# Low parts of the weights ahead of the experts: all made by VectorE (DVE), none by GpSimd

## The chip, the cores and the metric

The kernel runs on one core of one Trainium2 chip. The metric is the device time of one execution in microseconds (us). Before the change it is 2900.98 us, the median of 3 runs (2897.74 to 2901.92).

## The reference

Two transformer blocks are computed in fp32 on 256 tokens of width 2048. The first block is a Conformer-like mixer (convolution of width 31, chunked attention, attention to a memory) and a gated feed-forward layer with a short convolution. The second has four kinds of sparse attention and a mixture of 16 experts. Cut to the products with large weights:

```
proj = rmsnorm(x) @ w_in                       # 2048 x 12288
conv = silu(layernorm(dwconv31(a * sigmoid(g))))
merged = g0*(conv @ w_conv_out) + g1*(att @ w_attn_out) + g2*(memory @ w_mem_out)
h  = x + merged @ w_o
up = dwconv3(rmsnorm(h) @ w_up)                # 2048 x 11264
h  = rmsnorm(h + (silu(gt) * val) @ w_down)    # 5632 x 2048
mod = silu(c) @ ada_w + ada_b                  # one row, 2048 x 12288
y = h + g1 * (mixers(norm(h) @ w_in_2) @ w_out_2)
out = norm(y + g2 * experts(norm(y)))          # 16 experts, 2 chosen per token
```

## The kernel before

All weights (some 680 MB) are read once from HBM. TensorE (PE) multiplies in a fast fp32 format (`fp32r`), and the precision of fp32 is kept by splitting: a weight `w` becomes a high part `wh = fp32r(w)` and a low part `wl = w - wh`, an activation likewise `xh`, `xl`, and PE adds up the three products `wh*xh`, `wh*xl`, `wl*xh`.

A product (`Gemm`) is cut into chunks of 128 rows of the weight by up to 1024 columns. Two chunks come with one load of 1 MB, issued by SP into a ring of three buffers. `_split` makes the parts of a chunk: ScalarE (ACT) casts the high part (line 147), and then the low part is a subtraction of two tiles in SBUF (line 149; here called a sub). PE then runs the chunk's matmuls (`_mm`). With the weights as the stationary operand these are 24 matmuls, in lines 183, 184 and 185, the last of them the first to need the low part. In products of the other orientation (`tm`) they are lines 173, 174 and 175, of which 174 needs it.

The order of the work is written by `run`: chunks are split up to `AHEAD` = 4 chunks ahead of the one whose matmuls are issued next. After each chunk, `step` takes one item from each background queue: softmax pieces, convolution taps, evacuations in stages. Every engine runs its instructions in the order in which the program issues them. So the sub of a chunk stands on DVE between the background items of one step and those of the next.

Which engine runs the sub is decided by a counter, `nsplit`, and `pool_share`: every fourth sub of the first block goes to GpSimd (POOL), every third of the feed-forward layer and of the second block's projections, and none from `w_out_2` on (`pool_share` 999), so none in the experts.

Three kinds of work share DVE with the subs. The convolution of width 31 is 8 first taps (line 895) and 240 further ones (line 902), three to a step, each of two SBUF tensors and a column of factors. `ada_w_2` never reaches PE: 96 tiles of it are loaded beside the other weights and each is added up on DVE (line 1151). The feed-forward layer's short convolution (lines 1006 and 1007) and its gate (1046 on POOL, 1053 and 1058 on DVE) are stages of the queue `ev`. Lines 918 to 963 are the layer norm behind the convolution, and line 923 is a matmul of PE that waits for it.

Of the kernel before, what the change touches and what calls it, by code (L numbers as in the profile page):

```python
# [10 lines left out]
F32 = mybir.dt.float32  # L11
# [17 lines left out]
class Gemm:  # L29
# [6 lines left out]
    def __init__(self, w, x, evac, kts=None, cols=None, tm=False, before=None, after=None):  # L36
        self.w, self.x, self.evac, self.tm = w, x, evac, tm
        self.kts = list(range(w.shape[0] // 128)) if kts is None else list(kts)
        self.c0, self.c1 = cols if cols else (0, w.shape[1])
        self.C = self.c1 - self.c0  # L40
        self.before, self.after = before, after
        self.kk = max(1, 2048 // self.C)
        self.banks = None


class Kernel:
    def __init__(self, tc, ins, out, dbg=None):
        self.tc, self.nc, self.i, self.out, self.dbg = tc, tc.nc, ins, out, dbg or {}
        self.chunks, self.pos, self.split_pos, self.nsplit = [], 0, 0, 0
        self.side, self.every, self.count = deque(), None, 0  # L50
        self.rows, self.ahead_only = None, False
        self.loads, self.loaded = [], 0
        self.queues, self.reached = {}, set()
        self.n = 0
# [77 lines left out]
    def _split(self, c):  # L132
        n, off, width = c[:3]
        t, size = self.loads[n]
        wt = t[:, off:off + width]
        if c[3] is None:
            c[4](wt)
            self.free(t)
            return
        if c[7]:  # L140
            c[4], c[6] = wt, t
            return
        self.nsplit += 1
        c[6] = self.U(F32R)
        self.ahead += 1
        wh, wl = c[6][:, 0:1024], c[6][:, 1024:2048]
        self.nc.scalar.copy(wh[:, :width], wt)  # L147
        e = self.nc.gpsimd if self.nsplit % self.pool_share == 0 else self.nc.vector
        e.tensor_sub(wl[:, :width], wt, wh[:, :width].bitcast(F32))  # L149
        c[4], c[5] = wh, wl  # L150
        if off + width == size:
            self.free(t)

    AHEAD, pool_share = 4, 4

    def _mm(self, g, j, wh, wl):
        nc = self.nc
# [820 lines left out]
    def ffn(self):  # L978
# [7 lines left out]

        hid = {}
        NB = (DFF + 1023) // 1024
        self.every, self.pool_share = 3, 3
        self.nsplit = 0  # L990

        fw = i["ffn_conv_w"][0].rearrange("j (t p) -> (j t) p", p=128)
        for j in range(3):
# [254 lines left out]
    def after_ffn(self):  # L1248

        nc = self.nc  # L1250
        if "h1" in self.dbg:
            for tt in range(2):
                nc.sync.dma_start(self.dbg["h1"][tt * 128:tt * 128 + 128, :], self.h[tt])
        self.flush("ev")
        self.flush("norm")
        self.nsplit, self.pool_share = 2, 3
        for kt in range(0, 6, 2):
            self.turn1(kt)
        ss = self.small([128, 4], "ss4")
        nc.vector.tensor_reduce(ss, self.s2.rearrange("p (t k) -> p t k", t=4), axis=AX.X, op=OP.add)  # L1260

        v, zv = ss[:, 0:2], ss[:, 2:4]
        nc.vector.tensor_scalar(ss, ss, 1.0 / D, None, op0=OP.mult)
        nc.vector.tensor_scalar(v, v, EPS, None, op0=OP.add)
        nc.vector.scalar_tensor_tensor(zv, v, EPS, zv, op0=OP.mult, op1=OP.add)
        r = self.small([128, 16], "rstd", 3)
        nc.scalar.activation(r[:, 0:4], ss, AF.Sqrt)
        nc.vector.reciprocal(r[:, 0:4], r[:, 0:4])
        self.R2 = self.spread_tokens(r[:, 2:4])()
        self.parts1(0)  # L1270
        self.parts1(2)
        self.free(*self.h)
        self.free(self.fg)
        self.x = self.hf
        for tt in range(2):
            for c in range(0, D, 512):
                x = self.x[tt][:, c:c + 512]
                self.later("norm", 1 if tt + c else 9, lambda tt=tt, x=x: nc.gpsimd.tensor_scalar(x, x, r[:, tt:tt + 1], None, op0=OP.mult))
# [15 lines left out]
    def mixers(self):  # L1294
# [139 lines left out]
        def rows():  # L1434
            self.flush("ada")
            self.flush("norm")
            half(0)
            self.nsplit, self.pool_share = 0, 999
            self.lg = self.bank()

            self.ring.extend((self.NU, self.NU + 1))

        def begin(c0):
            part[0] = c0
            if c0 == 0:
                rows()
            elif c0 == 1024:
                half(1)

        def half(cb):  # L1450
            M[cb] = self.U()
            for n, k in enumerate((2, 4)):
                nc.gpsimd.dma_start(M[cb][:, n * 1024:n * 1024 + 1024],
                                    self.mod[k:k + 1, cb * 1024:cb * 1024 + 1024].to_broadcast([128, 1024]))
# [321 lines left out]
    def after_mix(self):  # L1776
# [21 lines left out]
        for tt in range(2):  # L1798
            e = slice(tt * 16, tt * 16 + 16)
# [61 lines left out]
        nc.vector.tensor_copy(self.most, most)  # L1861
        self.g2 = self.row(self.mod[5:6, :])
        self.resize(1)
        self.nsplit, self.pool_share = 0, 999

    def logits(self, kt):

# [489 lines left out]
```

## Time and profile before

| What | us |
|---|---|
| median of 3 runs | 2900.98 |
| the profiled execution | 2906.34 |
| its span, first to last instruction | 2904.5 |
| PE busy (matmul) | 2774.8 |
| DVE busy | 2159.3 |
| ACT busy | 1416.9 |
| POOL busy | 905.5 |

Busy times are those of the profiled execution. A matmul's end is modelled, so PE's busy share says where PE had no work rather than how near it is to its peak. Where PE has nothing to do, the view of waits names the line that waited, the line that ended the wait, the total in us, how often, and the longest. The granted clock of TensorE stands in the tables by stage as a share: 1.00 is 2.4 GHz and 0.50 is 1.2 GHz.

### The profile page before, as it was taken

The numbers are of one execution on the slowest core, as the hardware profiler recorded it, in microseconds if no ns is written. First come the engines' busy times: TensorE is split into PE (matmuls) and PEld (weight loads), VectorE is DVE, ScalarE is ACT, GpSimd is POOL, SyncE is SP. The second block draws the span as 40 slices with busy tenths as digits, with TensorE's granted clock in tenths as the row PEclk, the third lists the DMA queues.
The fourth block names the chain that finished last, engine by engine and source line by source line (L and its number), as shares of the span: only waits on it lengthen the run. The fifth ranks groups of instructions, "written<-read, shape, count | busy, mean of one in ns | idle before, by whom it ended". The sixth has DMA issues, their size and how long they took to land. (4 is left out here: it accounts for less than half of the span.)

```text
span 2904.5 us, 44128 instructions
## 1 busy us (share of the span) xinstructions
PE 2774.8 (96%) x17766; PEld 2423.2 (83%) x17766; DVE 2159.3 (74%) x2446; ACT 1416.9 (49%) x2100; POOL 905.5 (31%) x519
## 2 busy tenths in 40 slices
PE   8999999998999999999999999999999899999997
PEld 8898999988998899898989897997886676666664
DVE  5555559999766687887778776746545589998998
ACT  5434444333444444443434444435454476666665
POOL 3322322323344232333333342523221202222223
PEclk9999999999999999999999999989999899999999
DMA  7677654565567674676666674745564699989895
GB/s 253 203 264 233 220 198 163 179 216 198 209 237 270 213 269 171 210 268 215 250 215 249 232 239 156 247 153 191 171 212 154 211 341 340 344 328 343 324 344 212
DMA packets 201428, 685.78 MB, mean 236 GB/s; under 512 B 12147, under 2 KB 15331, under 8 KB 180355
## 3 DMA queue, kind: packets, MB, share of 16 engines
q1 hardware_dynamic: 194336, 662.94, 64.6%
q0 software_dynamic: 5680, 19.53, 2.6%
q8 instruction: 141, 2.31, 0.3%
q10 hardware_dynamic: 1203, 0.45, 0.1%
q14 instruction: 68, 0.56, 0.1%
HBM read 680.66 MB, written 2.20 MB: 235 GB/s over the span
## 5 line engine op out<-in xcount | busy, mean ns | idle before, releaser
L149 DVE TENSOR_TENSOR u<-u,u 128x1024 fp32r<-128x1024 f32 (+3 forms) x831 | 1117.7, 1374 | 406.0 <-ACT u L147 404.5
L147 ACT CAST u<-u 128x1024 fp32r<-128x1024 f32 (+3 forms) x1064 | 1014.3, 995 | 726.2 <-DMA u<-in_w_in_dram 252.4
L149 POOL TENSOR_TENSOR u<-u,u 128x1024 fp32r<-128x1024 f32 (+3 forms) x233 | 582.5, 2500 | 1116.5 <-ACT u L147 1008.4
L185 PE MATMUL ps<-u,u 128*128 128x256 f32 (+1 forms) x2184 | 623.4, 285 | 12.2 <-DVE u L149 9.7
L183 PE MATMUL ps<-u,u 128*128 128x256 f32 (+1 forms) x2184 | 628.3, 288 | 3.3 <-ACT u L147 2.7
L184 PE MATMUL ps<-u,u 128*128 128x256 f32 (+1 forms) x2184 | 622.7, 285 | 0.7 <-DVE u L1290 0.3
L185 PE MATMUL ps<-big,u 128*128 128x256 f32 (+1 forms) x1672 | 479.1, 287 | 17.1 <-DVE u L149 17.1
L183 PE MATMUL ps<-big,u 128*128 128x256 f32 (+1 forms) x1672 | 482.9, 289 | 1.2 <-ACT big L1289 0.7
L184 PE MATMUL ps<-big,u 128*128 128x256 f32 (+1 forms) x1672 | 477.9, 286 | 0.0
L185 PEld LDWEIGHTS ps<-u,u 128*128 128x128 f32 (+1 forms) x2184 | 422.3, 193 | 15.0 <-DVE u L149 11.7
L183 PEld LDWEIGHTS ps<-u,u 128*128 128x128 f32 (+1 forms) x2184 | 422.7, 194 | 12.6 <-issue 6.4
L184 PEld LDWEIGHTS ps<-u,u 128*128 128x128 f32 (+1 forms) x2184 | 422.8, 194 | 2.0 <-DVE u L1290 1.5
L185 PEld LDWEIGHTS ps<-big,u 128*128 128x128 f32 (+1 forms) x1672 | 324.6, 194 | 19.5 <-DVE u L149 19.3
L183 PEld LDWEIGHTS ps<-big,u 128*128 128x128 f32 (+1 forms) x1672 | 324.6, 194 | 13.4 <-issue 8.0
L184 PEld LDWEIGHTS ps<-big,u 128*128 128x128 f32 (+1 forms) x1672 | 324.6, 194 | 0.7 <-DVE big L1290 0.2
L1151 DVE SCALAR_TENSOR_TENSOR u<-u,cols,u 128x2048 f32<-128x2048 f32 x96 | 295.9, 3082 | 18.5 <-DMA u<-in_ada_w_dram 17.0
L174 PE MATMUL ps<-u,u 128*128 128x512 f32 x736 | 290.1, 394 | 15.8 <-DVE u L149 15.8
L173 PE MATMUL ps<-u,u 128*128 128x512 f32 x736 | 293.9, 399 | 1.5 <-ACT u L147 0.4
L175 PE MATMUL ps<-u,u 128*128 128x512 f32 x736 | 288.7, 392 | 0.0
L2135 POOL TENSOR_TENSOR u<-u,ev 128x512 f32<-128x512 f32 x56 | 116.3, 2090 | 418.6 <-DVE ev L2131 418.6
L1920 PE MATMUL ps<-u,xg 128*128 128x512 f32 x416 | 187.9, 452 | 0.4 <-DVE xg L1911 0.3
L174 PEld LDWEIGHTS ps<-u,u 128*128 128x128 f32 x736 | 139.6, 190 | 47.6 <-DVE u L149 20.3
(375 smaller groups left out, 3435.2 us busy)
## 6 DMA issues: line engine op xcount, KB each, us to landing
u<-in_w_in_dram SPq DMA_DIRECT2D x128, 1024.0 KB, 5.1
u<-in_ada_w_dram SPq DMA_DIRECT2D x96, 1024.0 KB, 6.0
u<-in_w_up_dram SPq DMA_DIRECT2D x88, 1024.0 KB, 6.3
u<-in_exp_w_gate_dram SPq DMA_DIRECT2D x64, 1024.0 KB, 9.4
u<-in_exp_w_up_dram SPq DMA_DIRECT2D x64, 1024.0 KB, 6.9
u<-in_exp_w_down_dram SPq DMA_DIRECT2D x64, 1024.0 KB, 8.2
u<-in_w_down_dram SPq DMA_DIRECT2D x44, 1024.0 KB, 6.8
u<-in_w_o_dram SPq DMA_DIRECT2D x16, 1024.0 KB, 6.9
```

Source lines behind the costliest of these rows:

```text
L147: self.nc.scalar.copy(wh[:, :width], wt)
L149: e.tensor_sub(wl[:, :width], wt, wh[:, :width].bitcast(F32))
L173: nc.tensor.matmul(o, xh[:, ts], wh[:, cs], start=first, stop=False)
L174: nc.tensor.matmul(o, xh[:, ts], wl[:, cs], start=False, stop=False)
L175: nc.tensor.matmul(o, xl[:, ts], wh[:, cs], start=False, stop=last)
L183: nc.tensor.matmul(o, wh[:, cs], xh, start=first and m % 2 == 0, stop=False, **kw)
L184: nc.tensor.matmul(o, wh[:, cs], xl, start=False, stop=False, **kw)
L185: nc.tensor.matmul(o, wl[:, cs], xh, start=False, stop=last, **kw)
L1151: nc.vector.scalar_tensor_tensor(a, wt, self.col["c"][:, kt:kt + 1], a, op0=OP.mult, op1=OP.add)
L1920: self.nc.tensor.matmul(ps, x, wh[:, s], start=start, stop=False)
L2135: nc.gpsimd.tensor_add(x, x, st["t"])
```

## The change

The counter, `pool_share` and the choice by them are gone. Every sub is issued on DVE, at the place in the program where it was issued on POOL before.

```diff
@@ _split
-        self.nsplit += 1
         c[6] = self.U(F32R)
         self.ahead += 1
         wh, wl = c[6][:, 0:1024], c[6][:, 1024:2048]
         self.nc.scalar.copy(wh[:, :width], wt)
-        e = self.nc.gpsimd if self.nsplit % self.pool_share == 0 else self.nc.vector
-        e.tensor_sub(wl[:, :width], wt, wh[:, :width].bitcast(F32))
+        self.nc.vector.tensor_sub(wl[:, :width], wt, wh[:, :width].bitcast(F32))
         c[4], c[5] = wh, wl
...
-    AHEAD, pool_share = 4, 4
+    AHEAD = 4
...
@@ ffn
-        self.every, self.pool_share = 3, 3
-        self.nsplit = 0
+        self.every = 3
```

The resets of the two numbers in `__init__`, `after_ffn`, `mixers` and `after_mix` go too. 233 subs move. Nothing else changes its engine or its place in the order. Lines behind the edit have numbers that are 2 to 6 smaller (the sub is line 147 after the change, a tap line 900).

DVE's order in the convolution of width 31, before: `u_4303` is the result that the taps add to, and the rows of line 149 are the subs of two chunks; the chunk between them is POOL's.

```order
L149 TENSOR_TENSOR u_5671<-u_5475,u_5671 128x1024
L902 SCALAR_TENSOR_TENSOR u_4303<-u_4280,cols_1361,u_4303 128x251
L902 SCALAR_TENSOR_TENSOR u_4303<-u_4280,cols_1361,u_4303 128x250
L902 SCALAR_TENSOR_TENSOR u_4303<-u_4280,cols_1361,u_4303 128x249
L902 SCALAR_TENSOR_TENSOR u_4303<-u_4280,cols_1361,u_4303 128x248
L902 SCALAR_TENSOR_TENSOR u_4303<-u_4280,cols_1361,u_4303 128x247
L902 SCALAR_TENSOR_TENSOR u_4303<-u_4280,cols_1361,u_4303 128x246
L149 TENSOR_TENSOR u_5733<-u_5537,u_5733 128x1024
```

The same place on DVE after the change:

```order
L147 TENSOR_TENSOR u_5671<-u_5475,u_5671 128x1024
L900 SCALAR_TENSOR_TENSOR u_4303<-u_4280,cols_1361,u_4303 128x251
L900 SCALAR_TENSOR_TENSOR u_4303<-u_4280,cols_1361,u_4303 128x250
L900 SCALAR_TENSOR_TENSOR u_4303<-u_4280,cols_1361,u_4303 128x249
L147 TENSOR_TENSOR u_5703<-u_5537,u_5703 128x1024
L900 SCALAR_TENSOR_TENSOR u_4303<-u_4280,cols_1361,u_4303 128x248
L900 SCALAR_TENSOR_TENSOR u_4303<-u_4280,cols_1361,u_4303 128x247
L900 SCALAR_TENSOR_TENSOR u_4303<-u_4280,cols_1361,u_4303 128x246
L147 TENSOR_TENSOR u_5733<-u_5537,u_5733 128x1024
```

The sub of `u_5703` stands between the two steps, three taps before it and three behind.

DVE's order in the feed-forward layer, before, ahead of a product with `w_down`: `u_11493` is an evacuated piece, `prob_11516` and `prob_11562` are pieces of the short convolution, `u_10461` the sum over `ada_w_2`.

```order
L1007 SCALAR_TENSOR_TENSOR prob_11516<-u_11493,fcw_1515,prob_11516 128x254
L149 TENSOR_TENSOR u_11542<-u_11426,u_11542 128x1024
L1006 SCALAR_TENSOR_TENSOR prob_11562<-u_11493,fcw_1672,prob_11562 128x255
L1007 SCALAR_TENSOR_TENSOR prob_11562<-u_11493,fcw_1515,prob_11562 128x254
L1006 SCALAR_TENSOR_TENSOR prob_11562<-u_11493,fcw_1672,prob_11562 128x255
L1007 SCALAR_TENSOR_TENSOR prob_11562<-u_11493,fcw_1515,prob_11562 128x254
L149 TENSOR_TENSOR u_11569<-u_11429,u_11569 128x1024
L1151 SCALAR_TENSOR_TENSOR u_10461<-u_11485,cols_1052,u_10461 128x2048
```

The same place on DVE after the change:

```order
L1004 SCALAR_TENSOR_TENSOR prob_11516<-u_11493,fcw_1515,prob_11516 128x254
L147 TENSOR_TENSOR u_11523<-u_11426,u_11523 128x1024
L147 TENSOR_TENSOR u_11542<-u_11426,u_11542 128x1024
L1003 SCALAR_TENSOR_TENSOR prob_11562<-u_11493,fcw_1672,prob_11562 128x255
L1004 SCALAR_TENSOR_TENSOR prob_11562<-u_11493,fcw_1515,prob_11562 128x254
L1003 SCALAR_TENSOR_TENSOR prob_11562<-u_11493,fcw_1672,prob_11562 128x255
L1004 SCALAR_TENSOR_TENSOR prob_11562<-u_11493,fcw_1515,prob_11562 128x254
L147 TENSOR_TENSOR u_11569<-u_11429,u_11569 128x1024
L147 TENSOR_TENSOR u_11584<-u_11429,u_11584 128x1024
L1148 SCALAR_TENSOR_TENSOR u_10461<-u_11485,cols_1052,u_10461 128x2048
```

Two subs (`u_11523`, `u_11584`) came from POOL, each next to a sub that DVE had already.

## Rows read from the trace of the kernel before

**Rows 1.** The page: busy us by engine, then DVE in 40 slices (tenths).

```profile
PE 2774.8 (96%) x17766; PEld 2423.2 (83%) x17766; DVE 2159.3 (74%) x2446; ACT 1416.9 (49%) x2100; POOL 905.5 (31%) x519
...
DVE  5555559999766687887778776746545589998998
```

**Rows 2.** Waits of PE, 585 to 770 us: who for whom: us, times, longest.

```profile
PE ps L185 <- DVE u L149: 18.6, 10, 6.3
PE ps L923 <- DVE ln L918: 5.5, 1, 5.5
PE ps L185 <- POOL u L149: 1.9, 1, 1.9
```

**Rows 3.** Waits of PE, 1115 to 1690 us.

```profile
PE ps L174 <- DVE u L149: 12.3, 10, 1.8
PE ps L185 <- DVE u L149: 6.4, 3, 2.6
```

**Rows 4.** By stretch: length, busy by engine, granted clock, DMA share, GB/s.

```profile
0.00:440.00 440.00, 431.64 (x3097) 400.50 (x3098) 246.06 (x290) 201.12 (x317) 131.73 (x99) 1.00 0.67 227
585.00:770.00 185.00, 158.56 (x1230) 155.52 (x1229) 169.53 (x175) 67.75 (x77) 59.37 (x26) 0.94 0.58 198
1115.00:1260.00 145.00, 135.24 (x900) 124.89 (x900) 120.27 (x108) 63.40 (x79) 50.53 (x23) 0.96 0.65 225
1850.00:2190.00 340.00, 334.80 (x2269) 297.44 (x2267) 187.05 (x391) 165.80 (x375) 103.10 (x89) 0.97 0.58 190
```

**Rows 5.** Stretches at half clock, first one and the sum of eight.

```profile
672.00:678.50 6.50, 3.99 (x18) 3.99 (x19) 6.39 (x6) 0.00 (x0) 4.69 (x2) 0.50 0.47 147
...
sum 32.30, PE 28.70 PEld 27.20 DVE 23.14 ACT 6.54 POOL 14.36; mean PE 3.59 PEld 3.40 DVE 2.89 ACT 0.82 POOL 1.80
```

**Rows 6.** Timeline of DVE, then of POOL: start us, us, line, count.

```profile
563.88 2.53 DVE L902 SCALAR_TENSOR_TENSOR u<-u,cols,u 128x255 f32<-128x255 f32 x1
...
567.47 1.50 DVE L902 SCALAR_TENSOR_TENSOR u<-u,cols,u 128x254 f32<-128x254 f32 x3
...
563.73 2.40 POOL L149 TENSOR_TENSOR u<-u,u 128x1024 fp32r<-128x1024 f32 x1 [1.94 <-ACT u L147]
```

**Rows 7.** Groups by line, 440 to 712 us: busy us, mean ns | idle before.

```profile
L902 DVE SCALAR_TENSOR_TENSOR u<-u,cols,u 128x255 f32<-128x255 f32 (+14 forms) x240 | 163.2, 680 | 6.4
L149 DVE TENSOR_TENSOR u<-u,u 128x1024 fp32r<-128x1024 f32 x57 | 75.0, 1318 | 0.0
...
L149 POOL TENSOR_TENSOR u<-u,u 128x1024 fp32r<-128x1024 f32 x29 | 78.1, 2694 | 182.4 <-ACT u L147 174.4 <-issue 7.9
```

**Rows 8.** Lines 902, 149 (0 to 2200 us), 1151: ns min/median/max.

```profile
L902 DVE SCALAR_TENSOR_TENSOR u<-u,cols,u x240: 449/470/2677, 440.9 to 705.4; 128x255 f32<-128x255 f32 x8, 128x253 f32<-128x253 f32 x8, 128x251 f32<-128x251 f32 x8, 128x249 f32<-128x249 f32 x8
L149 DVE TENSOR_TENSOR u<-u,u x480: 436/1220/3441, 8.4 to 2199.6; 128x1024 fp32r<-128x1024 f32 x139, 128x512 fp32r<-128x512 f32 x14, 128x280 fp32r<-128x280 f32 x4, 128x768 fp32r<-128x768 f32 x3
L1151 DVE SCALAR_TENSOR_TENSOR u<-u,cols,u x96: 2339/2350/4505, 143.4 to 2055.7; 128x2048 f32<-128x2048 f32 x96
```

**Rows 9.** Groups by line, 1115 to 1260 us.

```profile
L149 DVE TENSOR_TENSOR u<-u,u 128x1024 fp32r<-128x1024 f32 x33 | 52.7, 1623 | 15.7 <-ACT u L147 15.6
L1151 DVE SCALAR_TENSOR_TENSOR u<-u,cols,u 128x2048 f32<-128x2048 f32 x8 | 24.9, 3106 | 2.7 <-DMA u<-in_ada_w_dram 2.7
L1006 DVE SCALAR_TENSOR_TENSOR u<-u,fcw,u 128x255 f32<-128x255 f32 x8 | 8.1, 1016 | 0.0
...
L1006 DVE SCALAR_TENSOR_TENSOR prob<-u,fcw,prob 128x255 f32<-128x255 f32 x10 | 7.6, 762 | 5.3 <-ACT prob L1005 5.2
...
L149 POOL TENSOR_TENSOR u<-u,u 128x1024 fp32r<-128x1024 f32 x17 | 47.2, 2778 | 68.6 <-ACT u L147 56.7 <-DVE u L386 8.9 <-issue 3.1
```

**Rows 10.** Waits: DVE in 440 to 712 us, POOL whole span, SP in 440 to 712 us.

```profile
DVE u L447 <- ACT u L446: 0.5, 1, 0.5
...
POOL u L149 <- ACT u L147: 1008.4, 185, 18.0
...
SPq L128 <- DVE u L149: 198.9, 39, 11.5
```

More of the change, by code (lines that the diff above doesn't have):

```diff
@@ L48, in __init__ @@
         self.tc, self.nc, self.i, self.out, self.dbg = tc, tc.nc, ins, out, dbg or {}
-        self.chunks, self.pos, self.split_pos, self.nsplit = [], 0, 0, 0
+        self.chunks, self.pos, self.split_pos = [], 0, 0
         self.side, self.every, self.count = deque(), None, 0
@@ L1255, in after_ffn @@
         self.flush("norm")
-        self.nsplit, self.pool_share = 2, 3
         for kt in range(0, 6, 2):
@@ L1437, in rows @@
             half(0)
-            self.nsplit, self.pool_share = 0, 999
             self.lg = self.bank()
@@ L1863, in after_mix @@
         self.resize(1)
-        self.nsplit, self.pool_share = 0, 999
     def logits(self, kt):
```

## The prediction

> **What bounds the kernel now.** I read the page's busy times first, then the waits of PE by stretch, then the table by stretch with the granted clock, and last the timeline of DVE beside POOL. PE is busy for 2774.8 of 2904.5 us, so it is the engine that ends the kernel, and only time in which it waits, or runs at half clock, can be had back. DVE is second with 74%, but unevenly: its row of 40 slices reaches 9 in the slices of 500 to 700 us [rows 1]. That is the convolution of width 31.
>
> The waits of PE say where DVE is late. From 585 to 770 us PE waits 18.6 us in 10 waits for a sub on DVE, 1.9 us for a sub on POOL, and 5.5 us for the reduction of line 918: 26.0 us [rows 2], the same as the 26.4 us by which PE's busy time misses the stretch (185 less 158.56) [rows 4]. From 1115 to 1690 us, the feed-forward layer, it waits 12.3 us in line 174 and 6.4 us in line 185, both for subs of DVE: 18.7 us [rows 3].
>
> The clock comes on top. Eight stretches, from the one at 672 us to one at 1511.7 us, ran at a granted share of 0.50, which is 1.2 GHz; the first began while PE stood in its longest wait for a sub (6.3 us) and all others lie right behind a wait. PE was busy for 28.70 us in them, work that takes half as long at 2.4 GHz: 14.4 us lost [rows 5]. Four of the eight, 19.5 of their 32.3 us, lie in 585 to 770 us, so I put 8 us there and 6 in the feed-forward layer. (The mean clock of 0.94 over 158.56 us of work would say 9.5 us for the former [rows 4].) Everything that this change can reach is then 26.0 + 18.7 + 14.4 = 59 us.
>
> **The change: what a sub costs on either engine.** On DVE a sub of 128x1024 takes 1.22 us, the median of its line [rows 8]; on POOL it takes 2.69 us in the convolution and 2.78 us in the feed-forward layer [rows 7, 9]. 233 subs move. At 1.22 us each (some are narrower) that is at most 284 us more for DVE, a tenth of the span.
>
> But a sub on POOL isn't free for DVE. At 563.73 us POOL begins one that takes 2.40 us. The tap that DVE begins at 563.88 us takes 2.53 us; three taps at 567.47 us, with nothing on POOL, take 1.50 us together, 0.50 each [rows 6]. So DVE stood still for nearly all of POOL's sub, 2.0 us, which is more than the 1.22 us of doing it itself.
>
> Over the whole convolution (440 to 712 us): 240 taps have a mean of 680 ns and a median of 470, so 50 us is standing still; 57 subs on DVE have a mean of 1318 against 1220, another 6 us. POOL ran 29 subs meanwhile [rows 7, 8]. 56 us by 29 is 1.9 us of DVE's time for each sub that DVE did not do. Moving them takes 56 us away and adds 29 x 1.22 = 35 us: DVE has 21 us less to do.
>
> The Trainium skill ("SBUF — State Buffer", section "Who interferes with whom") says that DVE and GpSimd share one pair of SBUF ports as an exclusive lock, held for a whole instruction, and that a DVE instruction with two SBUF inputs contends with a GpSimd one that reads SBUF. The trace agrees in kind, and is smaller in size: 56 us where the whole of POOL's 78.1 us would be 100%. By the page the relief would be 78.1 - 35 = 43 us, the waits from 585 to 770 us would all go, and the kernel would end near 2858 us.
>
> **What that gives PE, from 585 to 770 us.** DVE has no idle time to lose there: from 440 to 712 us it waited for 0.5 us in all [rows 10], and its instructions stand in one queue, so what it saves goes straight to the subs for which PE waits. Of 26.0 us of waits I take 21 as gone, the relief of the convolution alone. What is late next is the reduction of line 918 behind the last taps: it follows them on the same queue and PE's line 923 waits for it, so I leave 5 us. With the long waits go the stretches at half clock: 6 of the 8 us. Sum: 27 us. Bounds: 15 us, if only the waits shrink and by two thirds of that; 34 us, if all waits and all the lost clock go.
>
> **The feed-forward layer, 1115 to 1690 us.** In 1115 to 1260 us 17 subs move and add 20.7 us. The 33 subs of DVE lose 33 x (1623 - 1220) = 13.3 us, the 8 additions of line 1151 lose 8 x (3106 - 2350) = 6.0 us, and line 1006 loses 8 x (1016 - 500) + 10 x (762 - 500) = 6.7 us, with 500 ns for a tap as wide [rows 6, 8, 9]. That is 26 us, of which some is due to POOL's products of line 1046, which stay. So DVE's load here is about even or a few us less. The gain is in lateness: a sub that POOL has is ready 2.78 us after it starts, and the DVE instruction that meets it is late by up to that (a sub took up to 3441 ns, an addition 4505 [rows 8]). I take half of what is there, 9 of 18.7 us and 3 of 6: 12 us. Bounds: 0 us, as the load is even, and 25 us.
>
> **Where the cover may go.** From 0 to 440 us and from 1850 to 2190 us the same swap is made, and DVE was idle there for 194 and 153 us [rows 4]. The moved subs lie in that idle time, though now and then one will stand in front of an evacuation or a softmax piece: I take 3 us lost. With the cover gone for a dozen of them it would be 12 x 1.22 = 15 us; 0 is the other end. From `w_out_2` on POOL had no subs, so nothing changes. Of the moved subs each now makes what stands behind it on DVE wait for ACT's cast: the next taps, the short convolution, the evacuations; that price is the third rival's below.
>
> **Sum.** 27 + 12 - 3 = 36 us. The profiled execution took 2906.3 us (span 2904.5 and 1.8 around it), so 2870. It lies 5.4 us above the median of the runs, 2901.0; from that I forecast 2865 us. With the ends of the terms, the likeliest case reaches from 2842 (all 59 us) to 2886 (15 us).
>
> **Rivals.**
>
> 1. The loads set the pace of the convolution, so that a faster DVE only waits for data. Then the 27 us are not there, 12 - 3 = 9 us remain: 2892 us. For it: SP, which issues the loads, waits a great deal. Against it: what SP waits for is DVE's subs, 198.9 us in 39 waits from 440 to 712 us, to have a buffer of the ring free [rows 10], and the DMA share of 585 to 770 us is 0.58, when 0.65 and 0.67 are reached elsewhere [rows 4].
>
> 2. Busy time is work: DVE is full in the convolution and 35 us more on it come out as 35 us more of PE's waiting, with some 15 us in the feed-forward layer, where DVE is busy for 120 of 145 us [rows 4]: 2951 us, slower. It decides from the point at which a sub on POOL costs DVE less than 1.22 us; the rows give 1.9 us. The Trainium skill ("Perfetto Trace Analysis", section "Identifying the Most-Contended Engine") speaks for it: occupancy, it says, is a fair measure for VectorE of how close the engine is to its roofline. By that rule an engine at 9 tenths would gain nothing by more work, and the trace disagrees: of the 163.2 us in which taps were busy, 50 were no work [rows 7, 8].
>
> 3. The waits for casts move to DVE and block its queue: slower. POOL waited 1008.4 us for ACT's casts in 185 waits, 5.5 us each [rows 10], at no cost, since nothing urgent stood behind. On DVE everything stands behind. In the feed-forward layer some 67 subs move (17 in 145 us, for 575 us). DVE's idle time there is 25 of 145 us, so 98 us. Were each held 2.2 us, that is 147 us, 49 more than there is idle: 2901 + 49 - 27 + 3 = 2926 us. It decides from about 1.8 us a sub, where it eats the other gain. Against it: DVE's own 33 subs waited 15.6 us for casts, 0.5 us each [rows 9], because an engine that is late finds the cast done.
>
> **Chances.** The forecast 0.74, the first rival 0.14, the second 0.05, the third 0.07. A measurement of this kernel can tell about 0.2%, 6 us, from no change. The forecast is faster by more than that all over its range; of the first rival I count two thirds as faster and the rest as no change: faster 0.83, same 0.05, slower 0.12. The range from 2842 to 2896 holds the forecast and most of the first rival, and leaves out the two slower cases.
>
> **What would show it.** Taps (line 900 after the change) with a mean near 480 ns in place of 680, and no tap of 2.5 us. DVE's busy time about the same as before, not 270 us more. PE's waits for line 147 between 585 and 770 us down from 20.5 us to a few; its wait in line 921 for the reduction (923 before) still there. The clock at 1.00 in most of that stretch. In the feed-forward layer fewer waits of line 172 (174 before). The first term is wrong if the taps are fast and PE still waits for subs; the whole is wrong if taps stay slow (then POOL's subs did not cause it), or if DVE shows waits for casts of over 2 us each in front of waits of PE.

## The result, and the profile after

The kernel after the change takes 2857.55 us, the median of 4 runs (2856.04 to 2860.09), against 2900.72 us of before beside it (2897.74 to 2901.92, 4 runs): 43.2 us less, a ratio of 0.9854 with a 95% interval of 0.9837 to 0.9871. The forecast was 2865 us. The two profiled executions differ by 50.3 us (2906.34 and 2856.04), since that of before lay 5.6 us above the median beside it and that of after 1.5 below; the working below goes by their spans, 2904.5 and 2854.3 us, 50.2 us apart.

The page of after, busy times and DVE's 40 slices, answers to [rows 1]:

```profile
PE 2756.7 (97%) x17766; PEld 2410.4 (84%) x17766; DVE 2106.4 (74%) x2679; ACT 1418.5 (50%) x2100; POOL 315.8 (11%) x286
...
DVE  5566558899767768877777786656555689998998
```

DVE has 233 instructions more and is busy for 53 us less. POOL is busy for 590 us less.

The groups by line from 440 to 694 us, the convolution, answer to [rows 7] (columns: busy us, mean ns | idle before); line 900 is the tap, line 147 the sub:

```profile
L900 DVE SCALAR_TENSOR_TENSOR u<-u,cols,u 128x255 f32<-128x255 f32 (+14 forms) x240 | 113.9, 475 | 5.7
L147 DVE TENSOR_TENSOR u<-u,u 128x1024 fp32r<-128x1024 f32 x86 | 104.6, 1219 | 6.8 <-ACT u L146 6.8
...
L893 DVE TENSOR_SCALAR u<-u,cols,cols 128x256 f32<-128x256 f32 x8 | 4.2, 531 | 0.0
```

The taps take 49.3 us less, all 86 subs take 29.6 us more than the 57 did, and line 893 (895 before, 7.4 us) 3.2 us less: 23 us less in all. Two taps are long now, with 1.24 and 1.40 us, and both lie beside an addition of 128x512 on POOL (line 619) that the change left there. In the trace of before the 26 taps of over 0.9 us all overlap an instruction of POOL, and the 202 taps beside which POOL did nothing took 485 ns at most. The view of the taps and of the additions over `ada_w_2`, over the whole span (ns min/median/max), answers to [rows 8]:

```profile
L900 DVE SCALAR_TENSOR_TENSOR u<-u,cols,u x240: 447/468/1395, 441.1 to 687.0; 128x255 f32<-128x255 f32 x8, 128x253 f32<-128x253 f32 x8, 128x251 f32<-128x251 f32 x8, 128x249 f32<-128x249 f32 x8
L1148 DVE SCALAR_TENSOR_TENSOR u<-u,cols,u x96: 2336/2346/3381, 144.7 to 2006.2; 128x2048 f32<-128x2048 f32 x96
```

The medians are where they were (470 and 2350 ns); the longest went from 2677 to 1395 and from 4505 to 3381 ns.

The timeline of DVE at the place of [rows 6] (start us, us, line, count):

```profile
562.80 1.22 DVE L147 TENSOR_TENSOR u<-u,u 128x1024 fp32r<-128x1024 f32 x1
563.93 1.50 DVE L900 SCALAR_TENSOR_TENSOR u<-u,cols,u 128x251 f32<-128x251 f32 x3
565.35 1.22 DVE L147 TENSOR_TENSOR u<-u,u 128x1024 fp32r<-128x1024 f32 x1
```

Where one tap had taken 2.53 us beside a sub on POOL, three taps take 1.50 us and the sub comes next.

The waits of PE for DVE from 560 to 760 us answer to [rows 2], the wait in line 183 there to that of line 185 before:

```profile
PE ps L921 <- DVE ln L916: 5.2, 1, 5.2
PE ps L183 <- DVE u L147: 4.7, 5, 1.2
```

And from 1080 to 1650 us, the feed-forward layer, to [rows 3] (line 172 was 174):

```profile
PE ps L171 <- ACT u L146: 5.3, 4, 1.3
PE ps L172 <- DVE u L147: 5.1, 8, 1.0
PE ps L183 <- DVE u L147: 0.5, 1, 0.5
```

The tables by stretch answer to [rows 4] (length, busy by engine, granted clock, DMA share, GB/s; the stretch has the matmuls that before had from 585 to 770 us), the stretch at half clock to [rows 5]:

```profile
584.70:746.60 161.90, 151.53 (x1229) 149.90 (x1229) 150.48 (x184) 64.59 (x74) 12.28 (x8) 0.98 0.62 215
...
690.50:696.50 6.00, 4.22 (x18) 4.07 (x19) 6.00 (x4) 0.96 (x2) 0.00 (x0) 0.50 0.65 226
```

In the convolution's stretch the granted clock went from 0.94 to 0.98. One stretch at 0.50 (1.2 GHz) is left there where four had been. It begins at 690 us, during the layer norm behind the last taps.

To place the gain I compared the times at which the two traces reach the same matmul, counted from the start:

| Stretch of before, us | Gain, us |
|---|---|
| 0 to 585 | 0.3 |
| 585 to 770 | 23.1 |
| 770 to 940 | 0.0 |
| 940 to 960 | 7.8 |
| 1115 to 1260 | 10.8 |
| the starts of three `w_down` products (1360 to 1400, 1505 to 1545, 1645 to 1690) | 1.9 + 1.8 + 1.8 |
| 1690 to 1950 | 4.7 |
| 1950 to 2190 | -2.2 |
| from 2190, the experts among them | 0 |

Two executions of one program differ as well. The run e3 below is the kernel before, instruction for instruction, and its trace runs within 0.7 us of that of before up to 1690 us, but is 5.5 us quicker from there to 1950 us. So the row from 1690 to 1950 us can't be put down to the change.

The place at 945 us is in none of the prediction's terms. It is the end of the product with `w_o`. The timeline of before there, DVE and then POOL (the bracket is the idle time ahead and what ended it):

```profile
942.15 4.17 DVE L1151 SCALAR_TENSOR_TENSOR u<-u,cols,u 128x2048 f32<-128x2048 f32 x1 [0.18 <-DMA u<-in_ada_w_dram]
946.23 2.47 DVE L658 TENSOR_TENSOR u<-u,ps 128x512 f32<-128x512 f32 x4
...
941.74 2.42 POOL L149 TENSOR_TENSOR u<-u,u 128x1024 fp32r<-128x1024 f32 x1 [4.21 <-ACT u L147]
```

The waits of PE of before, 940 to 960 us:

```profile
PE ps L356 <- DVE u L658: 6.0, 2, 5.3
```

The same place on DVE after the change:

```profile
914.38 2.35 DVE L1148 SCALAR_TENSOR_TENSOR u<-u,cols,u 128x2048 f32<-128x2048 f32 x1 [0.54 <-DMA u<-in_ada_w_dram]
916.65 2.47 DVE L656 TENSOR_TENSOR u<-u,ps 128x512 f32<-128x512 f32 x4
```

And the wait of PE there:

```profile
PE ps L354 <- DVE u L656: 0.2, 1, 0.2
```

A sub on POOL had made the addition of line 1151 1.8 us longer, right ahead of the four evacuations (line 658) that PE's next matmul waits for. That is the smaller part. Counted from the end of PE's last matmul ahead of the wait, the first evacuation began 4.6 us after it before and 1.6 us ahead of it after the change, which is 6.2 us. Of these, 4.4 us were already there when the addition began: the subs ahead of it waited for ACT's casts, which came later too. In e2 below the addition takes 2.35 us, and PE still waits 5.6 us here. That the moved subs cause the wait is shown by e7, which moves them up to here and gains 8.1 us at this place, and e8, which doesn't and gains 0.5; how they make the casts late wasn't tried.

The wait went from 6.0 to 0.2 us, and with it went a stretch at half clock that began in it:

```profile
945.00:951.80 6.80, 4.12 (x11) 3.20 (x12) 4.67 (x7) 4.31 (x11) 0.00 (x0) 0.50 0.87 283
```

### The profile page after: what moved, and what is told of

Its sections match the earlier page's. It is cut to its first block, busy times and chain, and to the rows that moved or that the text cites. A ratio compares the mean times of both kernels' runs of the same rounds, so it can differ in the third digit from the quotient of the medians.

```text
span 2854.3 us, 43859 instructions
## 1 busy us (share of the span) xinstructions
PE 2756.7 (97%) x17766; PEld 2410.4 (84%) x17766; DVE 2106.4 (74%) x2679; ACT 1418.5 (50%) x2100; POOL 315.8 (11%) x286
## 5 line engine op out<-in xcount | busy, mean ns | idle before, releaser
L147 DVE TENSOR_TENSOR u<-u,u 128x1024 fp32r<-128x1024 f32 (+3 forms) x1064 | 1258.1, 1216 | 393.9 <-ACT u L146 392.2
L181 PEld LDWEIGHTS ps<-big,u 128*128 128x128 f32 (+1 forms) x1672 | 322.9, 193 | 13.5 <-issue 7.0
L1148 DVE SCALAR_TENSOR_TENSOR u<-u,cols,u 128x2048 f32<-128x2048 f32 x96 | 226.3, 2357 | 5.6 <-DMA u<-in_ada_w_dram 5.5
L1914 PE MATMUL ps<-u,xg 128*128 128x512 f32 x416 | 187.9, 452 | 0.4 <-DVE xg L1905 0.3
L172 PEld LDWEIGHTS ps<-u,u 128*128 128x128 f32 x736 | 138.7, 188 | 39.4 <-DVE u L147 12.4
L171 PEld LDWEIGHTS ps<-u,u 128*128 128x128 f32 x736 | 138.5, 188 | 39.5 <-ACT u L146 8.7
L1915 PE MATMUL ps<-u,xg 128*128 128x512 f32 x416 | 167.7, 403 | 0.8 <-DVE u L147 0.7
```

Source lines behind the costliest of these rows:

```text
L147: self.nc.vector.tensor_sub(wl[:, :width], wt, wh[:, :width].bitcast(F32))
L171: nc.tensor.matmul(o, xh[:, ts], wh[:, cs], start=first, stop=False)
L172: nc.tensor.matmul(o, xh[:, ts], wl[:, cs], start=False, stop=False)
L181: nc.tensor.matmul(o, wh[:, cs], xh, start=first and m % 2 == 0, stop=False, **kw)
L1148: nc.vector.scalar_tensor_tensor(a, wt, self.col["c"][:, kt:kt + 1], a, op0=OP.mult, op1=OP.add)
L1914: self.nc.tensor.matmul(ps, x, wh[:, s], start=start, stop=False)
```

## The experiments

The theory: while a sub runs on POOL, DVE's instructions with two inputs in SBUF stand still, and this, not the place of the sub in a queue, made DVE late. Rivals: POOL's writes, not its reads, hold DVE up; a queue was late by the length of POOL's sub, whatever DVE does beside it; the gain comes from the feed-forward layer alone. Line numbers in an experiment are shifted by its edit; ratios are against the kernel before, timed on the same chip.

**e1: DVE makes all subs, and POOL reads beside it in short instructions.** In place of each moved sub of 512 columns or more POOL has eight subtractions of 80 columns of the high part, with a result that nobody reads.

```diff
-        e = self.nc.gpsimd if self.nsplit % self.pool_share == 0 else self.nc.vector
-        e.tensor_sub(wl[:, :width], wt, wh[:, :width].bitcast(F32))
+        self.nc.vector.tensor_sub(wl[:, :width], wt, wh[:, :width].bitcast(F32))
+        if self.nsplit % self.pool_share == 0 and width >= 512:
+            v = wh[:, :width].bitcast(F32)
+            for a in range(0, 640, 80):
+                self.nc.gpsimd.tensor_sub(self.waste, v[:, a % 400:a % 400 + 80], v[:, a % 400:a % 400 + 80])
```

> All subs are on DVE as in the changed kernel, and beside every one that POOL had before (widths 1024, 768 and 512) POOL runs eight subtractions of 80 columns of the high part, written to a tile that nobody reads; nothing waits for them but the reuse of the buffer. Theory (POOL's reads hold up DVE's two-input instructions): the taps' mean rises from 475 ns towards 680, DVE in the convolution gets the 35 us of the moved subs and the standing still as well, and the time is above the kernel before, 2900 to 2940 us. Rival (the gain came from subs being ready earlier on DVE, or from a shorter POOL queue): taps stay near 475 ns, 2858 us as in the changed kernel.

Measured: 2901.46 us (2897.52 to 2911.41), ratio 0.9994 (0.9984 to 1.0005). The groups of the whole span:

```profile
L153 POOL TENSOR_TENSOR waste<-u 128x80 f32<-128x80 f32 x1816 | 1198.7, 660 | 627.2 <-ACT u L148 495.0
...
L906 DVE SCALAR_TENSOR_TENSOR u<-u,cols,u 128x255 f32<-128x255 f32 (+14 forms) x240 | 117.9, 491 | 5.7
```

The time agrees with the theory and the reason does not. The taps have a mean of 491 ns, not 680, and 18.2 of the 23.4 us gained up to 770 us are still there. Of the 45 us by which e1 lags the kernel after, 20 are lost from 1950 to 2290 us: there the gain falls from 26.9 to 4.6 us, and PE waits for the softmax and DVE for its bias. POOL's queue issues the loads of that bias, and these stand behind its 1816 instructions. A wait of PE from 1950 to 2290 us, and then the page's group of the line that takes the bias (the last part says what ended the idle time before it):

```profile
PE ps L766 <- ACT prob L753: 12.8, 6, 5.6
```

```profile
L744 DVE CUSTOM_DVE_ANT_0 prob<-ps,bias 128x128 f32<-128x128 f32 x112 | 35.3, 352 | 44.8 <-PE ps L735 20.2 <-DMA bias<-scr 16.9 <-POOL waste L153 4.8
```

The other 25 us are 5 up to 770 us, 8.5 at 945 us, 8 in the feed-forward layer and 3 up to 1950 us. They weren't followed up; over the span ACT's casts waited 45.2 us for POOL's reads to free a buffer, which is a cost of the edit. So short reads are no replica of a long sub, and the run's time says nothing for the theory.

**e2: the same with writes.** ACT copies 80 columns, so that POOL starts when the chunk is there, and then POOL has twenty memsets of 80 columns.

```diff
+        if self.nsplit % self.pool_share == 0 and width >= 512:
+            self.nc.scalar.copy(self.waste, wh[:, 0:80].bitcast(F32))
+            for _ in range(20):
+                self.nc.gpsimd.memset(self.waste, 0.0)
```

> As e1, but POOL only writes: twenty memsets of 80 columns to a tile that nobody reads, after ACT has written the tile (so that they come at the same time as the subs did). If only reads of POOL hold DVE's second input, the taps stay near 475 ns and the time within 8 us of the changed kernel, 2850 to 2866 us. If any access of POOL to SBUF does, the taps rise to over 550 ns and the time lies near or above the kernel before, 2885 to 2940 us.

Measured: 2889.06 us (2884.86 to 2891.21), ratio 0.9945 (0.9929 to 0.9962). The time is the one expected if any access of POOL holds DVE up, the taps are those expected if only reads do. The groups of the whole span:

```profile
L153 POOL MEMSET waste<- 128x80 f32 x4540 | 749.3, 165 | 1011.0 <-ACT waste L151 762.2
L906 DVE SCALAR_TENSOR_TENSOR u<-u,cols,u 128x255 f32<-128x255 f32 (+14 forms) x240 | 114.9, 479 | 5.7
```

Up to 770 us the gain is whole (24.3 us) and the taps are at 479 ns, so POOL's short writes do not hold DVE up. As e1's short reads hardly do either, that alone doesn't tell reads from writes. The trace of the kernel after has long writes, six memsets of 128x2048 on POOL. Beside this one DVE makes two subs at their usual 1.2 us each (DVE, then POOL):

```profile
767.11 2.36 DVE L147 TENSOR_TENSOR u<-u,u 128x1024 fp32r<-128x1024 f32 x2 [0.58 <-ACT u L146]
...
767.01 1.82 POOL L1140 MEMSET u<- 128x2048 f32 x1 [22.67 <-PE ps L183]
```

Of the 34 us by which e2 lags the kernel after, 20 are lost from 1950 to 2290 us (the gain falls from 38.2 to 15.7 us). There DVE waits 14.4 us for the loads of the bias, as in e1, and ACT's copies wait 17.1 us for POOL. Another 7 us are the wait at 945 us, which e2 still has:

```profile
PE ps L360 <- DVE u L662: 5.6, 2, 4.9
```

**e3 and e4: one part of the change alone, first attempt.** In e3 only the number for the first block is set so high that POOL gets no sub, in e4 only those of the feed-forward layer and the second block.

```diff
-    AHEAD, pool_share = 4, 4
+    AHEAD, pool_share = 4, 999999      # e3
...
-        self.every, self.pool_share = 3, 3
+        self.every, self.pool_share = 3, 999999      # e4
...
-        self.nsplit, self.pool_share = 2, 3
+        self.nsplit, self.pool_share = 2, 999999      # e4
```

> Only the first block's subs move to DVE; from the feed-forward layer on POOL has every third, as before. By the traces the places of the first block (585 to 770 us and the end of w_o near 945 us) gave 31 of the 50 us between the two profiled executions: 31 us faster than before, 2866 to 2874 us. If the feed-forward layer carried the gain, 2890 us or more.

> The other half: the first block keeps every fourth sub on POOL, and from the feed-forward layer on all are on DVE. By the traces 19 of the 50 us: 2879 to 2888 us, and the gains of e3 and e4 add up to that of the whole change (within 5 us) if the places don't hand lateness on to one another. If the rest loses by itself (waits for casts on DVE), 2900 us or more.

Measured: e3 2904.34 us, ratio 1.0007 (0.9997 to 1.0017), which is the kernel before; e4 2855.43 us, ratio 0.9839 (0.9819 to 0.9859), which is the kernel after. Both expectations failed, and the reason is in the kernel: `ffn` sets its 3 while the list of products is made up, before `run` has split any chunk but the first. So POOL had every third sub of the first block, not every fourth, as was said above of the kernel before; the 29 of 86 subs of [rows 7] say the same. The prediction's counts are read from rows, so its sum doesn't hang on this. e7 and e8 set the number when the work gets there.

**e5 and e6: POOL reads in instructions as long as a sub.** DVE makes all subs, and in place of each moved one POOL subtracts the high part from itself, whole width, into a tile that nobody reads. Room for that tile comes from two pools of buffers, 3 in place of 4. e6 is the kernel after with these smaller pools alone.

```diff
+        if self.nsplit % self.pool_share == 0:
+            v = wh[:, :width].bitcast(F32)
+            self.nc.gpsimd.tensor_sub(self.waste[:, :width], v, v)      # e5
...
+        bufs = 3 if tag in ("prob", "pts") else bufs      # e5 and e6
```

> All subs on DVE, and POOL runs beside every third one a subtraction of its whole width (high part less high part) into a tile that nobody reads; the room for that tile comes from one buffer less of prob and of pts (as in e6). Theory (a POOL instruction that reads SBUF holds up DVE's two-input instructions for as long as it runs, so its length matters and not the total of POOL's work): taps with a mean near 680 ns again and single ones over 2 us, unlike the 491 ns of e1; in the convolution DVE has the 29 moved subs on top, so PE reaches the matmul that stood at 770 us before at 790 to 810 us; 2920 to 2965 us in all. Rival (POOL's work does not matter in itself): taps near 475 ns, that matmul at 747 us, time as e6.

> The changed kernel with 3 buffers of prob and of pts in place of 4: the control of e5. The buffers are reused at the earliest three steps later, after their last reader was issued, so at most a few us: 2855 to 2870 us, taps near 475 ns, the matmul of 770 us at 747 us.

Measured: e5 2963.43 us (2961.65 to 2965.21, 2 runs), ratio 1.0197 (1.0176 to 1.0217); e6 2856.03 us (2854.70 to 2857.36, 2 runs), 0.9827 (0.9807 to 0.9847). The matmul that before reaches at 770 us comes at 792.2 in e5 and at 748.3 in e6. The groups of e5 from 440 to 800 us:

```profile
L906 DVE SCALAR_TENSOR_TENSOR u<-u,cols,u 128x255 f32<-128x255 f32 (+14 forms) x240 | 147.4, 614 | 5.7
L149 DVE TENSOR_TENSOR u<-u,u 128x1024 fp32r<-128x1024 f32 x104 | 146.0, 1413 | 10.2 <-ACT u L148 10.2
...
L152 POOL TENSOR_TENSOR waste<-u 128x1024 f32<-128x1024 f32 x35 | 76.2, 2177 | 263.0 <-ACT u L148 263.0
```

And its timeline, DVE and then POOL, around one of them:

```profile
560.63 1.22 DVE L149 TENSOR_TENSOR u<-u,u 128x1024 fp32r<-128x1024 f32 x1
561.76 3.11 DVE L906 SCALAR_TENSOR_TENSOR u<-u,cols,u 128x241 f32<-128x241 f32 x3
564.79 1.22 DVE L149 TENSOR_TENSOR u<-u,u 128x1024 fp32r<-128x1024 f32 x1
565.93 1.46 DVE L906 SCALAR_TENSOR_TENSOR u<-u,cols,u 128x238 f32<-128x238 f32 x3
...
561.05 2.55 POOL L152 TENSOR_TENSOR waste<-u 128x1024 f32<-128x1024 f32 x1 [10.80 <-ACT u L148]
```

Nothing needs POOL's result here (over the whole span ACT waits 8.7 us for a buffer that POOL still reads), and DVE's order is that of the kernel after. Yet three taps take 3.11 us beside POOL's instruction and 1.46 us two steps on, where POOL is idle. In these 360 us DVE loses (147.4 - 113.9) + (146.0 - 104 x 1.219) = 53 us against the durations of after, 1.5 us for each of 35 instructions of POOL. That shows the theory's cause by itself: a long POOL instruction that reads SBUF costs DVE time. No sub of POOL stands in PE's way here, and PE still waits 24.1 us for DVE's subs from 440 to 800 us, so a queue that is late by the length of POOL's sub isn't needed for it. Put back alone, it turns the gain of 50 us that e6 has on this chip into a loss of 57. e6 shows that the buffers have no part in it. The times and the matmul came as the theory expected; the taps' mean, 614 ns, is short of the 680 expected.

**e7 and e8: one part of the change alone.** e7 has the moved subs on DVE up to the end of `w_o` and on POOL from there, up to `w_out_2`; e8 the other way round.

```diff
@@ after_o
+            self.nsplit, self.pool_share = 0, 3      # e7
+            self.pool_share = 999999      # e8
...
-        self.every, self.pool_share = 3, 3
+        self.every, self.pool_share = 3, 999999      # e7
...
-        self.nsplit, self.pool_share = 2, 3
+        self.nsplit, self.pool_share = 2, 999999      # e8
```

> e3 set the share while the program's products are listed, before any chunk is split, so that the feed-forward layer's setting overwrote it and e3 was the kernel before; here the switch is made when w_o ends. All subs on DVE up to there, every third on POOL behind. By the traces 31 us of gain lie before it: 2866 to 2876 us. If the earlier gain is given back in the feed-forward layer: 2885 us or more.

> The other half, switched at the same place: every third sub on POOL up to the end of w_o, all on DVE behind. 19 us of gain: 2878 to 2888 us; with e7 the gains add up to 43 us (within 6 us). If waits for casts on DVE cost anything in the feed-forward layer, 2890 us or more.

Measured: e7 2882.19 us (2878.13 to 2885.23), ratio 0.9917 (0.9900 to 0.9933), 24 us less than before; e8 2887.22 us (2886.09 to 2888.86), 0.9936 (0.9919 to 0.9952), 19 us less. Their sum is 43 us, where e6, timed on the same chip, gains 50. e8 came as expected. e7 was expected to be some 6 us faster at the least: up to 960 us it gains 31.4 us as it should, and then its feed-forward layer gives 7 us back (a gain of 33.2 us at 1260 and 26.1 at 1690, 24.5 at the end), with waits of PE for POOL from 1090 to 1680 us that the kernel before has not [rows 3]:

```profile
PE ps L174 <- POOL u L149: 11.5, 7, 2.2
PE ps L174 <- DVE u L149: 7.2, 4, 1.8
```

Its counter is set to 0 at another chunk than that of before, so POOL has other subs; whether that is why PE waits for them wasn't tried. The sum lacks 7 us, as many as e7 gives back, so e7's gain is a lower bound for its part of the change rather than its measure.

**e9: the rest of POOL's work on DVE too.** From the kernel after, three operations of half a chunk's width go to DVE: the gate's products (22), the sums of the branches (16) and the additions behind an expert (56).

```diff
-                    self.bg("ev", lambda: nc.gpsimd.tensor_add(m, m, t))
+                    self.bg("ev", lambda: nc.vector.tensor_add(m, m, t))
...
-                    nc.gpsimd.tensor_mul(L["g"], L["g"], S["val"][:, s])
+                    nc.vector.tensor_mul(L["g"], L["g"], S["val"][:, s])
...
-                nc.gpsimd.tensor_add(x, x, st["t"])
+                nc.vector.tensor_add(x, x, st["t"])
```

> The changed kernel with three more groups of POOL instructions on DVE, all 128x512: the gate products (22), the sums of the branches (16) and the experts' additions (56). In the trace of the changed kernel the DVE instructions that overlap them are longer than usual by 14, 11 and 40 us, 65 us in all; on DVE the 94 would take 0.68 us each, 64 us. Theory (only the balance of the two counts): no change, 2852 to 2863 us. If the gain came from taking work off POOL as such: some 10 us less, 2848 us or under; if DVE's queue is what limits it now: 2870 us or more.

Measured: 2834.43 us (2828.20 to 2838.03, 5 runs), ratio 0.9756 (0.9742 to 0.9771). No change was expected, and the time lies in the range given for work taken off POOL as such; it is the fastest version. Its span is 18.4 us shorter than that of after; 13.5 us of that come in the experts, where the change itself had gained nothing, and 7.8 in the feed-forward layer (of which 2.9 go again by 2290 us). In the experts, the timeline of after, DVE and then POOL:

```profile
2348.82 0.69 DVE L2125 TENSOR_TENSOR ev<-ps,u 128x512 f32<-128x512 f32 x1
2349.42 3.43 DVE L147 TENSOR_TENSOR u<-u,u 128x1024 fp32r<-128x1024 f32 x2
2352.78 0.68 DVE L2125 TENSOR_TENSOR ev<-ps,u 128x512 f32<-128x512 f32 x1
...
2349.59 2.18 POOL L2129 TENSOR_TENSOR u<-u,ev 128x512 f32<-128x512 f32 x1 [95.09 <-DVE ev L2125]
```

And that of e9 at the same place:

```profile
2343.87 0.68 DVE L2125 TENSOR_TENSOR ev<-ps,u 128x512 f32<-128x512 f32 x1
2344.47 2.35 DVE L147 TENSOR_TENSOR u<-u,u 128x1024 fp32r<-128x1024 f32 x2
2346.74 0.68 DVE L2129 TENSOR_TENSOR u<-u,ev 128x512 f32<-128x512 f32 x1
2347.34 0.68 DVE L2125 TENSOR_TENSOR ev<-ps,u 128x512 f32<-128x512 f32 x1
```

POOL's addition of 2.18 us made two subs 3.43 - 2.35 = 1.08 us longer. On DVE it takes 0.60 us from its start to the next one's. From one evacuation (line 2125) to the next there are 3.96 us with POOL and 3.47 without. This addition is one of the dearer: in the experts as a whole DVE's subs take 414.5 us after and 372.3 in e9, which is 0.75 us for each of the 56 additions, and DVE is busy for 538.7 us after and 529.3 in e9, additions included. So the two counts, 40 against 38 us in the expectation, were not even. Whether work off POOL counts besides, no run separates. A wait of PE in the experts, from 2240 us on, first after and then e9:

```profile
PE ps L1914 <- DVE ev L2125: 11.4, 6, 2.0
```

```profile
PE ps L1914 <- DVE ev L2125: 0.4, 1, 0.4
```

**e10: one more chunk split ahead.** The kernel after, whose waits for line 147 might come from a lead that is too short.

```diff
-                if c[3] is not None and not c[7] and self.ahead > self.AHEAD - (len(self.free_units) < 3):
+                if c[3] is not None and not c[7] and self.ahead > self.AHEAD + (len(self.free_units) > 5) - (len(self.free_units) < 3):
```

> The changed kernel, which may split one chunk more ahead where more than five buffers are free. What PE still waits for from 0 to 2200 us is casts and subs (lines 171, 172, 183: 19.5 us), as DVE and ACT answer each other in the gate's stages. If those are late for want of lead, up to 10 us less: 2847 to 2855 us. If they are late in a chain of its own, no change: 2855 to 2862 us.

Measured: 2854.18 us (2851.19 to 2855.64), ratio 0.9830 (0.9816 to 0.9843), where e4 and e6, which do what the kernel after does, have 0.9839 and 0.9827. The time lies at the edge of the range for a lead that is too short, but the intervals overlap: no effect of a longer lead is shown.

## Why the prediction was right, and where it was not

**The cause held.** A sub on POOL holds DVE up by more than the 1.22 us that it takes on DVE: 1.9 us in the prediction, and e5 shows a loss of 1.5 us for each of POOL's instructions with nothing else changed. The relief in the convolution was put at 21 us and came out as 23.

**585 to 770 us: predicted 27, measured 23.1 us.** PE's waits for subs fell from 20.5 to 4.7 us, so 16 us are gone where I took 21. That is the term that was mis-sized. The reduction behind the taps was put at 5 us and PE waits for it for 5.2 us. It is also where the half-clock stretch that is left begins. The clock was put at 6 us and gave 7: PE is busy for 151.5 us with the matmuls that took it 158.5.

**The feed-forward layer: predicted 12, measured 16.3 us.** The waits came out as forecast and the clock did not. The stretch with the same matmuls, of before and then of after:

```profile
1115.00:1690.00 575.00, 554.36 (x3780) 509.28 (x3780) 457.66 (x399) 245.32 (x309) 207.16 (x90) 0.99 0.67 231
```

```profile
1083.70:1642.40 558.70, 547.29 (x3781) 505.02 (x3780) 426.74 (x463) 246.51 (x309) 29.66 (x24) 1.00 0.66 238
```

PE had nothing to do for 20.6 us and has nothing to do for 11.4 us: 9.2 us less, where I took 9. Of 18.7 us of waits for subs 5.6 are left, and 5.3 us of waits for ACT's casts (line 171) stand where 1.0 had been. The clock was put at 3 us and gave 7.1, the fall of PE's busy time: 3.4 us ran at half clock in place of 13.7. DVE's load, put at "about even or a few us less", fell by 31 us. How much of the shorter waits comes from that, and how much from subs that are ready sooner, no run separates.

**Elsewhere: predicted -3, measured +2.5 us in the profiled pair.** Of the moved subs that stand in front of evacuations or softmax pieces a loss shows only from 1950 to 2190 us, 2.2 us; PE has nothing to do there for 6.3 us in place of 4.3, and in e4 likewise for 6.4. The 4.7 us gained from 1690 to 1950 us are mostly a difference between executions: e3, the same program as before, ran 13.7 us at half clock there, before ran 27.3 and after 20.5. By PE's idle time alone 1 to 2 us are gained there. The two stretches then about cancel.

**What was left out: 7.8 us at 945 us.** "Everything that this change can reach is then 26.0 + 18.7 + 14.4 = 59 us" is the sentence that failed. It counted PE's waits for subs and for the reduction only. The wait at 945 us is one for an evacuation, and POOL's sub had delayed the instruction in front of it by 1.8 us; late casts did the rest. Its list of half-clock stretches has the same gap: from 672 to 1515 us there are nine, not eight, and the one passed over is that at 945 us. The search should have been for every wait of PE on DVE with a POOL instruction beside it. One more sum was off: the low end of the likeliest case, 15 us, is the first term's alone, and with the low ends of all three terms it would be 15 + 0 - 15 = 0 us.

Against the profiled pair the four misses are -3.9, +4.3, +5.5 and +7.8 us, 13.7 of the 14.2 us by which the 50.2 us exceed the 36 of the sum. About 2.5 us of that are the difference between executions just told. In the runs' medians 43 us stand against 36: the forecast had taken off 5.4 us for the slower profile of before, and rightly so.

**The rivals.** That the loads set the pace is refuted by the DMA share of the convolution's stretch, which rose from 0.58 to 0.62 with the same matmuls. That busy time is work is refuted by DVE's own, 53 us less with 233 instructions more. The third, that waits for casts move to DVE and block it, can be read from DVE's waits, first before, then after:

```profile
DVE u L149 <- ACT u L147: 404.5, 253, 6.7
```

```profile
DVE u L147 <- ACT u L146: 392.2, 295, 6.7
```

There are 42 waits more and 12 us less of them; in the feed-forward layer, of which the rival spoke, 43 waits of 72.1 us became 51 of 63.4 us. The price that the rival put on moved casts did not fall due on DVE.

**The rule of an exclusive lock.** The figure of 2858 us, which the prediction got from the Trainium skill ("SBUF — State Buffer", section "Who interferes with whom"), is the measured time to a microsecond, but not by its reason. It took a relief of 43 us in the convolution, and that was 23; it took all waits from 585 to 770 us as gone, and 10.4 us of PE's idle time are left. The time came out alike, by luck, because of the 7.8 us at 945 us and the larger gain in the feed-forward layer. The same section states that a GpSimd instruction that only writes does not contend with a DVE instruction of two SBUF inputs; e2 agrees, with taps of 479 ns beside short memsets, and so does the kernel after, with subs of 1.2 us beside one of 1.82 us.

## What to carry to other kernels

An instruction given to a helper engine is priced by what its neighbours lose while it runs, not by what it takes off their count: compare the mean of an instruction with its median, and look at the timeline of both engines. Where the helper's instruction costs the busy engine more than its own would, take it back, first where the busy engine is late and right ahead of evacuations for which the matmul engine waits. In e9 DVE's busy time fell by 10.9 us (2106.4 and 2095.5 us), yet 18.4 us were gained, 11 of them in PE's waits for evacuations that came sooner.

## What the runs showed of the hardware

- Of the two lengths tried, DVE loses beside the long one and POOL beside the short one. Whole-width subtractions on POOL cost DVE 1.5 to 1.9 us each and take 2.2 to 2.8 us. Subtractions of 80 columns have a median of 322 ns and a mean of 660 in e1, while the taps have a mean of 491 ns where they have 475 without.
- Instructions of POOL that only write held no instruction of DVE up: in the kernel after six memsets of 1.8 us ran, the one shown in e2's section beside two subs, and every instruction of DVE beside them had its usual length.
- The loss falls on more than taps and subs. Line 895, with a single tensor from SBUF, took 2.4 to 2.5 us in the two of eight cases that began beside a sub of POOL, and 0.41 us in the others.
- Evacuations with one input in PSUM kept their length beside POOL: of the 48 additions of line 1074 before, the 28 that ran beside an elementwise instruction of POOL took 0.67 to 0.69 us, like the 19 that ran beside none.
